# Row sums on one core: the early load of eight rows per partition split in one and seven

## The chip, the cores and the metric

The kernel runs on one core of one Trainium2 chip. The metric is the device time of one execution in microseconds; lower is better. Before the change it is 160.62 us, the median of 3 runs (160.59 to 160.69). The profile comes from one execution of its own.

## The reference

```python
def setup_inputs():
    batch, seq, dim = 32, 512, 1024
    return {"x": np.random.randn(batch, seq, dim).astype(np.float32)}

def reference(x):
    return np.sum(x, axis=-1).astype(np.float32)
```

The input is 16,384 rows of 1,024 float32 (67.1 MB), the output one sum per row (64 KB). There is one addition per element read, so the work is above all reading.

## The kernel before, in words

Each of the 128 partitions gets 128 rows of 4 KB: 16 from the first region of the input (`x_a`) and 112 from the second (`x_b`), consecutive in memory within a region. The rows of a partition are counted from 0 to 127; `rows_from(j, n)` gives rows j to j+n-1 of all partitions. There are three buffers of 16 rows per partition (64 KB), `rows_0` to `rows_2`.

**The loads.** The first one is the early load: rows 112 to 119, eight per partition, 4 MB, into the first half of `rows_0`. It is issued by SyncE (SP, L97). Then follow seven loads of 16 rows per partition (8 MB each, rows 0 to 111), issued by GpSimd (POOL, L99) with `single_packet=True`. The first two of these go into the other two buffers and need no wait; from the third on, POOL waits at L153 until VectorE has summed the buffer that is to be filled again. The last eight rows, 120 to 127, come by four closing loads, again from POOL (L179), cut so that rows 5 and 7 are divided at odd places: `five` has 22,416 B per partition, `seventh` 7,192 B, `sixth` 2,160 B and `eighth` 1,000 B. The pieces `sixth` and `eighth` land in a small tile, `ends`.

**The early load's place.** `issue_first_load_at_entry` (L9 to L27) runs when the program is finalized. It looks for the first DMA that SP issues, takes it out of its block and puts it into the program's entry block, ahead of SP's first drain, which is where the barriers between all engines begin. So this one DMA is issued before the barriers; everything else in the kernel stands behind them. The function moves exactly one DMA and requires that it has no wait.

**The sums.** VectorE (DVE) sums the early load's eight rows and then six of the loads of 16 rows with one `tensor_reduce` each (L106, in `vec`), each behind a wait for that load's semaphore (L172), and each raises `summed`. The seventh load of 16 is shared: DVE sums ten rows with `halves` (L115), a custom instruction that adds the two halves of a row and accumulates, and ScalarE (ACT) sums six with `activation` and its accumulator (L135). The closing rows are shared likewise. ACT stores the sums of the finished rows early (L210, L211), and SP stores the last 16 per partition when DVE's `done` and ACT's `acts` are there (L225 to L227).

**What sets the order.** The order on each engine is that of the program text; there is no scheduler and no pool. DMA transfers of SP go into one queue and those of POOL into another; both are served by the same 16 DMA engines. Each load has a semaphore of its own, which 16 engines raise by one each when their part has landed, so a wait for a whole load is a wait for 16.

Of the kernel before, what the change touches and what calls it, by code (L numbers as in the profile page):

```python
# [30 lines left out]
def kernel(  # L31
# [5 lines left out]
    nc = tc.nc  # L37
# [12 lines left out]
    BIG = 16  # L50
# [15 lines left out]
    def rows_from(j, n):  # L66
        if j < ONE:
            return x_a[:, j : j + n, :]
        return x_b[:, j - ONE : j - ONE + n, :]

    last = J // BIG - 1
    tail = last * BIG
    FIRST = 8
# [14 lines left out]
    def semaphore(name):  # L88
        return ctx.enter_context(nc.semaphore(name=name))

    def block_of(t, a, n):
        return t[:, a * dim : (a + n) * dim].rearrange("p (n d) -> p n d", d=dim)

    def load(dst, src, k):
        sem = semaphore(f"load_{k}")
        if k == "first":
            nc.sync.dma_start(out=dst, in_=src).then_inc(sem, 16)  # L97
        else:
            nc.gpsimd.dma_start(out=dst, in_=src, single_packet=True).then_inc(sem, 16)  # L99
        return sem  # L100

    summed = semaphore("summed")
# [1 line left out]
    def vec(j, block):  # L104
        n = block.shape[1]
        return nc.vector.tensor_reduce(  # L106
            out=sums[:, j : j + n],
            in_=block,
            axis=mybir.AxisListType.X,
            op=mybir.AluOpType.add,  # L110
        )
# [32 lines left out]


    t = bufs[0]
    block = block_of(t, 0, FIRST)
    landed = load(block, rows_from(tail, FIRST), "first")
    loads = [(landed, tail, block)]
    for g in range(last):  # L150
        t = bufs[(1 + g) % 3]
        if g > 1:
            nc.gpsimd.wait_ge(summed, g - 1)  # L153
        block = block_of(t, 0, BIG)
        loads.append((load(block, rows_from(g * BIG, BIG), g), g * BIG, block))

# [2 lines left out]
    j = tail + FIRST  # L161
    t = bufs[(1 + last) % 3]
# [5 lines left out]
    whole6, whole8 = ends[:, :six], ends[:, six:]  # L168
    right6, right8 = whole6[:, 1:-1], whole8[:, 1:-1]
    nc.vector.memset(ends[:, six - 1 :: whole8.shape[-1]], 0.0)  # L170
    for landed, first, block in loads[:-1]:
        nc.vector.wait_ge(landed, 16)  # L172
        vec(first, block).then_inc(summed, 1)
    nc.gpsimd.wait_ge(summed, last - 1)
    line = rows_from(j, 8).rearrange("p n d -> p (n d)")
# [1 line left out]
            (right6, 5 * dim + SIXTH), (right8, 7 * dim + EIGHTH))  # L177
    five, seventh, sixth, eighth = (
        load(dst, line[:, at : at + dst.shape[-1]], f"run_{k}")  # L179
        for k, (dst, at) in enumerate(runs)  # L180
    )
# [3 lines left out]

    paired = semaphore("paired")
    carried = semaphore("carried")
    landed, first, block = loads[-1]
    n_pairs = 10
    nc.vector.wait_ge(landed, 16)  # L190
    for q in range(n_pairs):
# [67 lines left out]
```

## Time and profile before

| | |
|---|---|
| runs (median, lowest, highest) | 160.62 us, 160.59 us, 160.69 us |
| profiled execution, its own time | 160.88 us |
| its span, from SP's first issue to the end of SP's wait for the last store | 159.6 us |
| DVE busy | 121.6 us (76%) |
| ACT busy | 11.0 us (7%) |
| POOL busy | 6.2 us (4%) |
| early load, issue to landing | 24.5 us |
| DVE's first reduce (8 rows), start and length | 24.48 us, 8.7 us |
| DVE's later reduces (16 rows), length of each | 17.2 us |

The span is what the profile's instructions cover; the execution's own time is 1.3 us longer than the span. A load's time from issue to landing contains the time that its packets stand behind others, so it is not the time that the transfer would take alone: the loads of 16 rows need 40.5 us (median) by this count while two of them are under way. Beside the page, the trace holds a record of each instruction, of each DMA packet (queue, start, length, size; not which of the 16 engines moved it) and of each time that a semaphore was raised.

### The profile page before, as it was taken

Reading aid. Unit: us, or ns where it says so; the run is one execution under the profiler, and the core shown is the slowest. Engines: PE = TensorE matmul, PEld = TensorE weight load, DVE = VectorE, ACT = ScalarE, POOL = GpSimd, SP = SyncE. Lnnn points to the kernel's source line nnn. Section 1 sums busy time; section 2 is a strip of 40 time slices with the busy share of each in tenths; the row PEclk is TensorE's granted clock in tenths of the full one; section 3 lists DMA queues with packets and bytes.
Section 4 is the critical chain, followed back from the end, with each engine's and each line's share of the span. In section 5 each row is a group of like instructions: output and inputs, shape, how many; then the busy total and the mean of one; then the engine's idle time right before and its main releaser. Section 6 shows DMA issues by size and latency. Waiting matters only on the chain.

```text
span 159.6 us, 123 instructions
## 1 busy us (share of the span) xinstructions
DVE 121.6 (76%) x42; ACT 11.0 (7%) x19; POOL 6.2 (4%) x15
## 2 busy tenths in 40 slices
DVE  0000008999998999949999499986999679995986
ACT  3000000000000000000000000000000000000995
POOL 3000000010001000010000100010000220000000
DMA  7999996996997979969969969969969979898993
GB/s 263 526 394 394 435 600 279 526 509 279 526 444 345 526 345 444 526 279 509 526 263 526 526 263 526 509 279 526 509 279 526 460 329 526 378 411 364 438 402 127
DMA packets 2000, 67.18 MB, mean 421 GB/s; under 512 B 624, under 2 KB 624, under 8 KB 848
## 3 DMA queue, kind: packets, MB, share of 16 engines
q0 software_dynamic: 1424, 62.92, 91.2%
q1 hardware_dynamic: 288, 4.20, 6.6%
q10 hardware_dynamic: 288, 0.06, 0.2%
HBM read 67.11 MB, written 0.07 MB: 421 GB/s over the span
## 4 chain that ended last, share of the span: by engine, by line
DMA 74%; DVE 22%; POOL 1%; issue 1%; POOLq 0%
DMA rows<-in_x_dram 56%; DVE sums L106 22%; DMA ends<-in_x_dram 19%; POOL rows L99 1%; DVE ends L115 0%; DVE sums L115 0%; POOLq L43 0%
## 5 line engine op out<-in xcount | busy, mean ns | idle before, releaser
L106 DVE TENSOR_REDUCE sums<-rows 128x16 f32<-128x16384 f32 (+1 forms) x7 | 111.9, 15999 | 32.2 <-DMA rows<-in_x_dram 32.2
L135 ACT ACTIVATE unread<-rows 128x1024 f32<-128x1024 f32 x9 | 9.1, 1013 | 145.5 <-DMA rows<-in_x_dram 145.5
L115 DVE CUSTOM_DVE_ANT_0 rows<-rows 128x512 f32<-128x512 f32 (+2 forms) x15 | 9.0, 659 | 2.6 <-DMA rows<-in_x_dram 2.6
L99 POOL DMA_DIRECT2D rows<-in_x_dram x9 | 4.9, 546 | 122.4 <-DVE sums L106 120.9
L135 ACT ACTIVATION_READ_ACCUMULATOR unread<-rows 128x1 f32 x9 | 1.7, 186 | 0.0
L135 ACT ACT_TABLE_LOAD x1 | 1.3, 1283 | 1.4 <-PEq L43 1.4
L170 DVE MEMSET ends<- 128x2 f32 x1 | 0.1, 60 | 1.5 <-PEq L43 1.5
L115 DVE DVE_READ_ACCUMULATOR2_ANT sums<- 128x1 f32 x15 | 1.2, 80 | 0.0
L99 POOL DMA_DIRECT2D ends<-in_x_dram x2 | 1.1, 543 | 0.0
L115 DVE CUSTOM_DVE_ANT_0 ends<-ends 128x271 f32<-128x271 f32 (+1 forms) x2 | 0.7, 364 | 0.1
L115 DVE DVE_READ_ACCUMULATOR2_ANT ends<- 128x1 f32 x2 | 0.2, 84 | 0.0
L243 POOL MEMSET const-float32-0.0<- 128x1 f32 x1 | 0.1, 99 | 0.2 <-issue 0.2
L243 POOL MEMSET const-bfloat16-1.0<- 128x1 bf16 x1 | 0.1, 103 | 0.0
L243 POOL MEMSET const-float32-1.0<- 128x1 f32 x1 | 0.1, 99 | 0.0
L243 POOL MEMSET const-uint8-127<- 128x1 uint8 x1 | 0.1, 99 | 0.0
## 6 DMA issues: line engine op xcount, KB each, us to landing
rows<-in_x_dram SPq DMA_DIRECT2D x1, 4096.0 KB, 24.5
rows<-in_x_dram POOLq DMA_DIRECT2D x1, 2802.0 KB, 27.9
rows<-in_x_dram POOLq DMA_DIRECT2D x1, 899.0 KB, 29.6
ends<-in_x_dram POOLq DMA_DIRECT2D x1, 270.0 KB, 29.7
ends<-in_x_dram POOLq DMA_DIRECT2D x1, 125.0 KB, 29.5
rows<-in_x_dram POOLq DMA_DIRECT2D x7, 40.5
out_dram<-sums ACTq DMA_DIRECT2D x1, 48.0 KB, 1.6
out_dram<-sums ACTq DMA_DIRECT2D x1, 8.0 KB, 1.5
```

Of the source, the lines that this page charges most:

```text
L99: nc.gpsimd.dma_start(out=dst, in_=src, single_packet=True).then_inc(sem, 16)
L106: return nc.vector.tensor_reduce(out=sums[:, j : j + n], in_=block, axis=mybir.AxisListType.X, op=mybir.AluOpType.add,)
L115: return nc.vector.tensor_tensor_reduce(out=src[:, :n], in0=src[:, :n], in1=src[:, n:], scale=1.0, scalar=0.0, op0=mybir.AluOpType.add, op ...
L135: nc.scalar.activation(out=unread[n_acts % len(unread)][:, :], in_=src, func=mybir.ActivationFunctionType.Copy, accum_out=sums[:, j : j + ...
L170: nc.vector.memset(ends[:, six - 1 :: whole8.shape[-1]], 0.0)
L243: nc = _bacc.Bacc("TRN2", target_bir_lowering=False, num_devices=1)
```

## The change

SP's early load becomes two loads on SP: the first of the eight rows per partition (512 KB), and the other seven (3.5 MB). `issue_first_load_at_entry` is unchanged, and it moves only the first DMA of SP; so the load of one row is issued in the entry block ahead of the barriers, and the load of seven rows stands at the head of SP's part of the kernel, behind them. Both raise one semaphore, `entry`, and DVE's first reduce waits for 32 instead of 16. The destination, the rows and the order of everything else are the same; the later loads stay POOL's.

```diff
     def load(dst, src, k):
         sem = semaphore(f"load_{k}")
-        if k == "first":
-            nc.sync.dma_start(out=dst, in_=src).then_inc(sem, 16)
-        else:
-            nc.gpsimd.dma_start(out=dst, in_=src, single_packet=True).then_inc(sem, 16)
+        nc.gpsimd.dma_start(out=dst, in_=src, single_packet=True).then_inc(sem, 16)
         return sem
...
     t = bufs[0]
-    block = block_of(t, 0, FIRST)
-    landed = load(block, rows_from(tail, FIRST), "first")
-    loads = [(landed, tail, block)]
+    entry = semaphore("entry")
+    for j, n in ((0, 1), (1, FIRST - 1)):
+        nc.sync.dma_start(out=block_of(t, j, n), in_=rows_from(tail + j, n)).then_inc(entry, 16)
+    loads = [(entry, 32, tail, block_of(t, 0, FIRST))]
     for g in range(last):
...
-        loads.append((load(block, rows_from(g * BIG, BIG), g), g * BIG, block))
+        loads.append((load(block, rows_from(g * BIG, BIG), g), 16, g * BIG, block))
...
-    for landed, first, block in loads[:-1]:
-        nc.vector.wait_ge(landed, 16)
+    for landed, count, first, block in loads[:-1]:
+        nc.vector.wait_ge(landed, count)
         vec(first, block).then_inc(summed, 1)
...
-    landed, first, block = loads[-1]
+    landed, _, first, block = loads[-1]
```

## Prediction

> **What bounds the kernel now.** I began with the page's table of DMA queues, to see how much of the span the 16 DMA engines are at work:
>
> ```profile
> q0 software_dynamic: 1424, 62.92, 91.2%
> q1 hardware_dynamic: 288, 4.20, 6.6%
> q10 hardware_dynamic: 288, 0.06, 0.2%
> HBM read 67.11 MB, written 0.07 MB: 421 GB/s over the span
> ```
>
> The shares add up to 98.0% of 159.6 us, so all that is not transfer is 3.2 us. q1 is SP's queue (the early load, and the last store), q0 is POOL's. Next the busy time by stretches, to see where those 3.2 us lie (a row: stretch, length, DVE, ACT, POOL, clock, DMA share, GB/s; a transfer counts where it begins):
>
> ```profile
> 0.00:1.00 1.00, 0.00 (x0) 0.00 (x0) 0.20 (x4) 1.00 0.00 0
> 1.00:25.00 24.00, 0.58 (x2) 1.28 (x1) 1.20 (x2) 1.00 1.04 437
> 25.00:50.00 25.00, 25.00 (x2) 0.00 (x0) 0.53 (x1) 1.00 0.97 419
> 50.00:100.00 50.00, 44.95 (x4) 0.00 (x0) 1.59 (x3) 1.00 1.02 440
> 100.00:150.00 50.00, 43.60 (x10) 2.16 (x5) 2.65 (x5) 1.00 0.99 427
> 150.00:157.00 7.00, 6.51 (x23) 6.62 (x14) 0.00 (x0) 1.00 0.94 394
> 157.00:160.00 3.00, 0.98 (x6) 0.90 (x2) 0.00 (x0) 1.00 0.13 23
> ```
>
> They lie in the first microsecond and the last three; in between no engine is ever without work. The chain of work that ended last says the same by its last pieces:
>
> ```profile
> 127.69 29.73 DMA ends<-in_x_dram
> 157.42 0.02 issue
> 157.44 0.04 DVE ends L115
> 157.48 0.33 issue
> 157.81 0.08 DVE sums L115
> ```
>
> Compute follows the last landings within some tenths. The kernel is thus a fixed number of bytes per engine behind a start: it ends when the engine that started last has moved its 4.19 MB. For that start I read the trace's DMA packet records. One of SP's packets is one partition's piece (32,768 B); each of 16 engines has eight, and one closing packet of 4 B that raises the semaphore. The 16 first packets begin 1.02 to 1.54 us after SP's issue at 0.00. They take long, 1.47 to 2.36 us, and end at 2.90 to 3.21 us on 15 engines, at 3.52 on one. From the second on, each takes 1.213 to 1.232 us. So the start-up costs an engine, beyond its first 1.213 us, 1.68 to 1.99 us, and 2.30 us on the last one. That one never catches up: the last of each load's 16 landings is 0.31 to 0.35 us behind the one before it, from the first load (24.46 us against 24.13) to the final one (157.76 against 157.41). **That engine sets the end**, and the others have 0.3 us and more to spare.
>
> The start on the instruction side, by the timeline's first 3 us:
>
> ```profile
> 0.00 0.38 SPq L97 DMA_DIRECT2D rows<-in_x_dram  x1
> ...
> 1.44 1.28 ACT L135 ACT_TABLE_LOAD   x1 [1.44 <-PEq L43]
> 1.51 0.06 DVE L170 MEMSET ends<- 128x2 f32 x1 [1.51 <-PEq L43]
> 1.94 1.20 POOL L99 DMA_DIRECT2D rows<-in_x_dram  x2 [1.50 <-POOLq L43]
> ```
>
> SP issues before the barriers, the others act after them. SP's last barrier event ends at 1.375 us. POOL's first load, issued at 1.94, has its first packet at 6.54 us, so until then only SP's load feeds the engines: four of its packets on each.
>
> **The change, part by part.**
>
> *The packets.* Eight of 32,768 B (8 x 1.213 = 9.70 us per engine) become eight of 4,096 B and eight of 28,672 B, with one more closing packet (9 ns). Neither size occurs before. Near 4,096 B stand 4,320 B at 170 ns and 3,000 B at 127 ns (the closing loads): by the line between them 162 ns. Between 22,416 B (837 ns) and 32,768 B (1,213 ns) a 28,672 B packet takes 1,064 ns. Sum: 8 x 0.162 + 8 x 1.064 + 0.009 = 9.82 us, **+0.12 us** on every engine. If the cost went by bytes alone, at the large packets' rate, it would be 0.01; I take 0.12, since the neighbouring sizes measure it.
>
> *The second issue.* In the changed kernel's order of instructions SP has the 128x1024 copy, the branch with the barriers, the 128x7168 copy, the store: so the change does what it says. The copy's wait is the barrier's, and SP has nothing behind it until the store at 158 us, so nobody queues. Its issue comes at 1.375 us plus a step that the trace has no row for on SP. ACT's step from its last barrier event to its table load is 0.06 us, DVE's to its memset 0.12, POOL's to its first DMA 0.61 (POOL is the far end, as it prepares packets itself). I take ACT's, the other queue that issues through hardware: **1.44 us**. The issue itself, 0.35 to 0.46 us in the four hardware-queue rows, is off the path, as the packets' delay already runs from its beginning.
>
> *Does the entry row cover the way to the second load?* The entry row keeps an engine busy for 1.30 us past its start-up: to 2.98 to 3.29 us on 15 engines, **3.60 us on the last**. The second load flows, with the first load's own delays, at 1.44 + 1.68 to 1.99 = 3.12 to 3.43 us. The 15 could stand idle for some 0.14 us, which their 0.3 us of slack takes up. The last one is covered if its extra 0.31 us are not repeated. I hold that they are not: stretches of one first packet (1.85 to 2.15 us on most, 2.36 there) show once in the trace and at no later change of load or queue. If they are, its data come at 1.44 + 2.30 = 3.74 us and 0.14 us are lost. Below: SP's and ACT's stores have their first packets 0.85 to 0.95 us after issue instead of 1.02, which closes the gap. I take **0**; the ends are a loss of 0.14 us with ACT's step and of 1.98 + 2.30 - 3.60 = 0.68 us with POOL's.
>
> *The start-up itself.* It is the first packet's stretch beyond 1.213 us: 0.64 us on a typical engine, 1.15 on the last. Is it tied to the packet's size? The trace has no second start with idle engines and a load. I take no change, as the cost then is one of time; the closing loads' small packets, 23.5 to 26 B/ns, say that small ones flow no faster. The bound below: with no stretch, the entry row is through at 1.54 + 1.30 = 2.84 us at the latest, and the second load takes over at 1.44 + 1.54 = 2.98 us instead of 3.60: a gain of 0.62 us.
>
> *What else moves.* The first reduce waits for both loads (count 32). They hold the same bytes in the same queue, so it starts near 24.5 us as before. Behind it is POOL's third load at 33.46 us, whose bytes are wanted only when the second ends at 50.4 us; with the 4.6 us from POOL's issue to its first packet there are 12 us of cover. The barriers may come some hundredths earlier if SP's entry issue shrinks; POOL's packets are wanted much later, so that is worth nothing.
>
> *The sum.* 0.12 + 0 + 0 = +0.12 us. On the profiled execution (span 159.58, its time 160.88, 1.30 of it around the span) that is 161.00 us. It ran 0.26 above the median of the runs, and the median carries the forecast: 160.62 + 0.12 = **160.74 us**.
>
> **The rivals.**
>
> *A: the engines run dry behind the entry row (slower).* One mechanism, at the seam near 3 us: SP's second issue is late, or its first packets stretch like the first load's, with only 1.30 us of work in front. It decides when the second load's data reach the latest engine after 3.60 us, that is with an issue after 1.30 us if that engine is slow again, after 1.61 us if the slow 1.99 us of the others hold. With POOL's step it loses 0.68 us: 160.62 + 0.12 + 0.68 = 161.42 us; halfway, 161.1. For it: before, four packets stood there, now one eighth of the load. Against it: ACT's 0.06 us, and the slack of 15 engines. Chance 0.20.
>
> *B: small first packets shorten the start-up (faster).* If a stretch belongs to the large first packet, up to 0.62 us go: 160.62 + 0.12 - 0.62 = 160.12 us. If only the one engine falls in line with the rest, 0.31 go: 160.43. For it: the stretch is seen on first packets only. Against it: nothing shows it to be size and not the cold start. The part of it under 160.30 I give 0.15.
>
> *C: each load pays a fixed cost of its own.* If the second load's packets moved only once the first's completion is through, the last engine would wait from 3.60 us for the 0.35 us between closing packet (first at 23.46) and landing (23.81) and then stretch again by 0.64 to 1.15: +1.0 to 1.5, 161.7 to 162.2 us. Against it: the closing load of 7,192 B per partition lands 2.21 us behind the one before it, and its eight packets of 0.276 us are 2.21 us: nothing is between them. Chance 0.04. The Trainium skill, "DMA: Bandwidth & Descriptors", section "Anatomy of one DMA — SWDGE (gpsimd) path", fits a DMA's time with a constant of about 2.0 us beside its bytes, and its section "Rules for kernel authors" wants at least 1 MiB per DMA, which the 512 KB entry row is not; an estimate that adds that constant once would be about 162.7 us. The trace's 2.21 us speak against adding it for loads that stand queued behind one another.
>
> **How the numbers follow.** 0.2% is 0.32 us, about what a measurement of this kernel can tell from no change; the bounds are 160.30 and 160.94. The forecast has 0.61, from 160.43 (the one engine in line) to 160.88 (its slow start repeated). Slower is A and C, 0.24; faster is B, 0.15. The range reaches into both until a tenth is left out at each end: 160.25 to 161.10 us.
>
> **What would show it.** Right: 16 engines with no idle time between the last 4,096 B packet and the first of 28,672 B; those packets at 0.16 and 1.06 us; SP's second issue at about 1.44 us; the final landing some 0.12 us later. A shows as idle time on the latest engine at 3 to 4 us, and as every landing later by it; B as first packets that take under 0.5 us and landings earlier than 157.76 us; C as idle time of 0.3 us and more on all 16. Wrong altogether would be a change after 30 us, in the closing loads or the stores: there I expect the same intervals as before.

## The result, and the profile after

The changed kernel takes 163.07 us (median of 5 runs, 162.87 to 163.23) against 160.62 us for the kernel before (160.57 to 160.69): a ratio of 1.0153, 95% interval 1.0138 to 1.0167. It is slower by 2.45 us, where 0.12 us had been forecast. The profiled execution took 163.13 us, with a span of 161.8 us.

The table of DMA queues of the changed kernel (packets, MB, share of 16 engines over the span):

```profile
q0 software_dynamic: 1424, 62.92, 90.0%
q1 hardware_dynamic: 432, 4.20, 6.9%
q10 hardware_dynamic: 288, 0.06, 0.2%
HBM read 67.11 MB, written 0.07 MB: 415 GB/s over the span
```

The bytes are the same. The shares add up to 97.1% of 161.8 us, so 4.7 us are without transfer where there were 3.2 us: 1.5 us of idle time are new. The transfers themselves take 157.1 us of an engine instead of 156.4 us: 0.7 us are new there, in packets that take longer. By these shares POOL's queue has 145.6 us in both kernels, so most of the 0.7 us lies in SP's packets.

The chain's last pieces, and the stretches (columns as above):

```profile
129.99 29.68 DMA ends<-in_x_dram
159.66 0.02 issue
159.69 0.04 DVE ends L112
159.72 0.33 issue
160.05 0.08 DVE sums L112
```

```profile
1.00:25.00 24.00, 0.06 (x1) 1.28 (x1) 1.20 (x2) 1.00 1.01 412
25.00:50.00 25.00, 15.96 (x2) 0.00 (x0) 0.53 (x1) 1.00 0.97 422
50.00:100.00 50.00, 50.00 (x4) 0.00 (x0) 1.59 (x3) 1.00 1.01 436
100.00:150.00 50.00, 45.67 (x3) 0.00 (x0) 2.65 (x5) 1.00 0.99 427
```

The end is the old one, 2.3 us later: the same DVE steps behind the same last landing, 160.02 us against 157.76. From 25 us on the engines move as much as before; up to there they move 412 GB/s instead of 437. By the landings: the first load of 16 rows has landed 2.47 us later (34.18 against 31.71), the next 2.30 us (53.36 against 51.06), and the final one 2.26 us. So everything was lost before 32 us, and nothing later.

The start, by the timeline, and the two new loads in the list of DMA issues (KB, us from issue to landing):

```profile
0.00 1.75 SPq L146 DMA_DIRECT2D rows<-in_x_dram  x2
...
1.43 1.28 ACT L132 ACT_TABLE_LOAD   x1 [1.43 <-PEq L43]
1.50 0.06 DVE L168 MEMSET ends<- 128x2 f32 x1 [1.50 <-PEq L43]
1.93 1.20 POOL L96 DMA_DIRECT2D rows<-in_x_dram  x2 [1.49 <-POOLq L43]
34.04 8.69 DVE L103 TENSOR_REDUCE sums<-rows 128x8 f32<-128x8192 f32 x1 [32.48 <-DMA rows<-in_x_dram]
```

```profile
rows<-in_x_dram SPq DMA_DIRECT2D x1, 3584.0 KB, 32.6
rows<-in_x_dram SPq DMA_DIRECT2D x1, 512.0 KB, 3.5
```

The 1.75 us are two issues of 0.36 and 0.33 us with the barriers between them; the second begins at 1.42 us, as forecast (1.44). The row lands 3.5 us after its issue. The seven rows land 32.6 us after theirs. DVE's first reduce starts 9.6 us later for that (34.04 us instead of 24.48), and it costs nothing: DVE then reduces without a pause until 111 us and has caught up.

What happens in between shows first in the stretch from 3 to 4 us (columns as above; a transfer counts where it begins), in the kernel before and then in the changed one:

```profile
3.00:4.00 1.00, 0.00 (x0) 0.00 (x0) 0.15 (x1) 1.00 0.84 360
```

```profile
3.00:4.00 1.00, 0.00 (x0) 0.00 (x0) 0.13 (x1) 1.00 0.28 90
```

Few transfers begin there in the changed kernel, 90 GB/s instead of 360. The packet records tell more. The row's closing packets come at 2.73 to 3.22 us. The first packets of the seven rows come at 2.73 to 3.22 us on five engines, and at 3.9 to 4.9 us on the others. So most engines stand idle, for 0.8 to 2.2 us, and their first packet of 28,672 B then takes up to 0.93 us longer than the 1.062 us of the later ones. (The records don't name the engine; which packets follow one another on one engine is worked out from their times.) I sum this up for each run by two numbers, worked out from the packet records: idle time, and stretch (what packets took beyond the time of their size in the stream), both from 0 to 32 us and as a mean of the 16 engines. The idle time of the kernel before is the way to the first packets.

| kernel | idle | stretch | sum | last landing |
|---|---|---|---|---|
| before | 1.1 us | 0.7 us | 1.8 us | 157.76 us |
| changed | 2.3 us | 1.4 us | 3.7 us | 160.02 us |

The sum is 1.9 us more. The rest of the 2.26 us is spread: the final load's first and last landing lie 1.85 us apart (158.17, 160.02), before 0.65 us, and the last one counts.

### The profile page after: what moved, and what is told of

The parts are those of the page before. It is cut to its first block, busy times and chain, and to the rows that moved or that the text cites. A ratio compares the mean times of both kernels' runs of the same rounds, so it can differ in the third digit from the quotient of the medians.

```text
span 161.8 us, 124 instructions
## 1 busy us (share of the span) xinstructions
DVE 121.3 (75%) x42; ACT 11.0 (7%) x19; POOL 6.2 (4%) x15
## 4 chain that ended last, share of the span: by engine, by line
DMA 60%; DVE 37%; POOL 1%; issue 1%
DMA rows<-in_x_dram 41%; DVE sums L103 37%; DMA ends<-in_x_dram 18%; POOL rows L96 1%; DVE ends L112 0%; DVE sums L112 0%
## 6 DMA issues: line engine op xcount, KB each, us to landing
rows<-in_x_dram SPq DMA_DIRECT2D x1, 3584.0 KB, 32.6
```

## The experiments

The runs were made in four jobs. Each job ran the kernel before beside its kernels, and the ratios are to that. The theories have numbers or letters that hold for the run at hand; they are not the rivals A, B and C of the prediction.

**First job: the split, the place, the cover, the company.** The theories were: (1) the one row is too little work to cover the second load's way; (2) the split itself costs; (3) the second load is slowed by POOL and ACT, which start beside it.

*Both loads at the entry (e1).* The helper moves SP's first two DMAs, not the first alone.

```diff
-        at = next((k for k, i in enumerate(insts) if isinstance(i, mybir.InstDMACopy) and i.engine == SP), None)
+        at = [k for k, i in enumerate(insts) if isinstance(i, mybir.InstDMACopy) and i.engine == SP][:2]
...
-        main.instructions = entry[:k] + [load] + entry[k:]
+        main.instructions = entry[:k] + loads + entry[k:]
```

> One row and seven rows as in the changed kernel, but both of SP's loads stand in the entry block, so the second is issued behind the first at about 0.4 us and not behind the barriers. Theory 1 (the one row covers 1.3 us of work, and the second load's first packets come up to 2.7 us or more after an issue at 1.42 us, with a stretch of 0.4 to 0.95 us on top): the second issue is a microsecond earlier, its packets are there when the row is through (2.7 to 3.2 us) on nearly all engines, 160.4 to 161.0 us. Theory 2 (two loads, small packets or the shared semaphore cost this wherever they stand): about 163 us. Theory 3 (the second load is slow because it starts while POOL writes its packets and ACT loads its table, 1.4 to 3.1 us): 160.4 to 161.0 us, as theory 1.

Measured 160.56 us, ratio 0.9997 (0.9988 to 1.0006). The timeline:

```profile
0.00 0.84 SPq L143 DMA_DIRECT2D rows<-in_x_dram  x2
...
2.40 1.20 POOL L93 DMA_DIRECT2D rows<-in_x_dram  x2 [1.96 <-POOLq L40]
```

The second issue ends at 0.84 us, the barriers come 0.5 us later for it, and POOL's first load with them (2.40 instead of 1.93); that costs nothing. The first packets of the seven rows come at 2.5 to 3.25 us and follow the row's without a gap. So the split, the sizes and the shared semaphore cost nothing. Theory 2 is out.

*Nothing at the entry (e2).* The kernel before without the line `nc.at_finalize(issue_first_load_at_entry)`.

> The kernel before, but its eight-row load is left in its place behind the barriers. Theory 1 (what costs is a seam behind a short first load): there is no seam; everything starts 1.42 us later, 160.62 + 1.42 = 162.0 us, which is better than the changed kernel. Theory 2 (the split costs): also 162.0 us. Theory 3 (a load issued at 1.4 us is slow because of what runs beside it): first packets at 2.7 to 4.9 us instead of 2.4 to 3.0, 163 us or more.

Measured 162.03 us, ratio 1.0085 (1.0071 to 1.0099). SP issues at 1.39 us, beside the table load at 1.40:

```profile
1.39 0.38 SPq L96 DMA_DIRECT2D rows<-in_x_dram  x1
1.40 1.28 ACT L134 ACT_TABLE_LOAD   x1 [1.40 <-PEq L42]
```

All 16 first packets begin at 2.39 to 2.81 us, 1.0 to 1.4 us after the issue, and their stretch is 0.70 us, as with the early load. A load issued at 1.4 us to idle engines is not slow. And the row that the changed kernel loads early gains it nothing: without any early load this kernel is no slower.

*Four rows and four (e3).*

```diff
-    for j, n in ((0, 1), (1, FIRST - 1)):
+    for j, n in ((0, 4), (4, FIRST - 4)):
```

> The changed kernel with four rows at the entry and four behind the barriers. Theory 1: four rows are about 5 us of work per engine, to 6.6 us or later, and the second load's packets are there by 4.9 us at the latest: no idle time, 160.6 to 160.8 us. Theory 2: about 163 us. Theory 3: the second load may be slow, but four rows cover it, 160.6 to 160.8 us.

Measured 160.63 us, ratio 1.0000 (0.9991 to 1.0009). There is no idle time behind the start. With four rows in front, the barriers' place does no harm.

*POOL's first load behind the row's landing (e4).* SP's two loads get a semaphore each, DVE waits for both, and

```diff
+        if g == 0:
+            nc.gpsimd.wait_ge(row, 16)
```

> The changed kernel with a semaphore for each of SP's two loads, and POOL's first load waits until the one row has landed (3.5 us), so that POOL writes no packets while the second load starts. POOL's packets are still in time, as seven rows keep the engines busy for 8 us. Theory 1: no change from the changed kernel, 162.8 to 163.3 us. Theory 2: the same. Theory 3, as far as POOL's issue is what runs beside it: the second load's first packets at 2.4 to 3.1 us on all engines, 160.6 to 161.3 us.

Measured 162.26 us, ratio 1.0101 (1.0087 to 1.0115). That is 0.8 us less than the changed kernel in its own job, so I took POOL's issue for a part of the cause, although the first packets of the seven rows still came as late as some 4.2 us, with 0.7 us of new idle time. The last job shows that this was wrong.

**Second job: which delay?** Theory A: a load issued while the engines move data needs 2.5 us and more to its first packets. Theory B: the packets arrive in time, but SP's queue, running empty, takes them up in a second start.

*Four rows by ACT (e5).*

```diff
-    for j, n in ((0, 1), (1, FIRST - 1)):
-        nc.sync.dma_start(out=block_of(t, j, n), in_=rows_from(tail + j, n)).then_inc(entry, 16)
+    for issuer, j, n in ((nc.sync, 0, 4), (nc.scalar, 4, FIRST - 4)):
+        issuer.dma_start(out=block_of(t, j, n), in_=rows_from(tail + j, n)).then_inc(entry, 16)
```

> Four rows at the entry by SP, the other four behind the barriers by ACT, whose queue is another one: the 16 engines take turns between the two queues, so the first packet of ACT's load shows when its packets have arrived while SP's packets flow. Theory A (any load issued while the engines are moving data needs 2.5 to 3.5 us to its first packet): first packets at 3.9 to 4.9 us. Theory B (packets arrive within 1.0 to 1.5 us as always, but a queue that is just running empty takes them up only in a second start): 2.4 to 3.2 us, up to 0.6 us later by the packet that is under way. The time is that of the kernel before in both, 160.5 to 160.8 us.

Measured 160.57 us, ratio 0.9997 (0.9987 to 1.0006). ACT issues at 1.43 us, and its first packets come from 5.1 us on, up to 6.3 us: 3.7 to 4.9 us after the issue, in a queue of its own, while the packets of the other queue (0.61 us each) follow one another. Theory B as it stood is out; the delay is even longer than theory A had it. The engines had packets of SP to move all the while (no idle time), so this run can't tell late packets from packets that stand in line.

*Seven rows by ACT (e6).* As e5, with one row and seven.

> One row at the entry by SP, the seven others behind the barriers by ACT, in a queue that has not run before. Theory A: as the changed kernel, first packets of the seven rows at 2.7 to 4.9 us, 162.5 to 163.3 us. Theory B: first packets at 2.4 to 3.2 us, little idle time, 160.6 to 161.3 us.

Measured 161.93 us, ratio 1.0087 (1.0072 to 1.0102). First packets from 2.6 us on, 0.5 us of new idle time. Another queue doesn't heal the seam; the time fits neither expectation.

*Two rows and six (e7).* The pairs are (0, 2) and (2, 6).

> The changed kernel with two rows at the entry and six behind the barriers: the two rows keep the engines busy to 4.0 to 4.4 us. Theory A: packets of the second load arrive at 2.7 to 4.9 us, so idle time of 0 to 0.6 us on some engines, 160.6 to 161.5 us. Theory B: the packets are there well before the queue runs empty, no idle time, 160.5 to 160.8 us.

Measured 161.86 us, ratio 1.0088 (1.0064 to 1.0111): above both ranges. The six rows' first packets come from 3.8 us on, with a mean of 0.25 us of idle time, and the stretch sums to 1.1 us.

*The seven rows issued only when the row has landed (e8).*

```diff
+        if j:
+            nc.sync.wait_ge(row, 16)
```

> The changed kernel with a semaphore for each of SP's loads, and SP issues the seven rows only when the one row has landed (3.25 us), that is 1.8 us later, at engines that stand idle. Theory A: a load that is issued to idle engines has its first packets after 1.0 us, at 4.3 to 4.6, with a stretch of 0.6 us; so the later issue costs little, 162.5 to 163.3 us, the changed kernel's time. Theory B: the same, as the changed kernel's second load makes a second start too. If instead the changed kernel's loss were the lateness of its issue alone, 1.8 us would be added, 164.9 us.

Measured 161.85 us, ratio 1.0074 (1.0058 to 1.0091), below both ranges. The timeline says what fills the gap:

```profile
0.00 3.53 SPq L148 DMA_DIRECT2D rows<-in_x_dram  x2
...
1.95 1.20 POOL L96 DMA_DIRECT2D rows<-in_x_dram  x2 [1.51 <-POOLq L43]
```

SP's second issue now comes at 3.2 us. POOL's first load, issued at 1.95 us as ever, with nothing in front of it but the rest of the one row (through by 2.9 us), has its first packets at 3.33 to 4.17 us, 1.4 to 2.2 us after its issue; before the change, behind eight rows, they came at 6.54 to 7.16 us, 4.6 to 5.2 us after it. SP's seven rows are now behind POOL's load: they begin at 8.8 us, 5.6 us after their issue, when each engine has moved two of POOL's 64 KB packets. So POOL's 4.6 us were for the most part not POOL's own: they were the wait behind the load in front. Since POOL's load had been issued before SP's second one, the run doesn't show what a second load of SP needs with nothing in front of it; e15 below does.

**Third job: the dose, and the delay away from the start.**

*Three rows and five (e9).*

> The changed kernel with three rows at the entry and five behind the barriers. One row lost 2.45 us and two rows 1.23 us, a difference of 1.22 us, which is one more row's work; so the second load takes over at the same moment, some 5.3 us, whatever stands in front (theory A: a load issued while the engines move data needs that long). Three rows end near 5.3 us: nothing or 0.1 us is lost, 160.6 to 160.8 us. Theory B (every seam in SP's queue with the barriers in between costs a start of its own) gives a third loss of some 0.6 us, 161.2 us.

Measured 160.55 us, ratio 0.9995 (0.9986 to 1.0004), with no idle time. Three rows are enough. So, by the medians and by rows at the entry, the loss is: none 1.5 us (e2), one 1.7 to 2.5, two 1.2, three 0.

*Seven rows by ACT and POOL late (e10)*, the edits of e6 and e4 together.

> One row at the entry by SP, seven behind the barriers by ACT, and POOL's first load waits until the one row has landed: the two changes that each took part of the loss away (0.8 us and 1.1 us), together. Theory C (POOL's issue beside it and SP's queue still running are two separate delays of the second load): both parts go, some 161.2 us. Theory A (a load issued into running transfers is late whatever the queue, and what is left is the second start): no better than the better of the two alone, 161.8 to 162.0 us.

Measured 162.10 us, ratio 1.0093 (1.0077 to 1.0108). The two supposed parts don't add: it is 0.1 us above theory A's range, and 0.9 us above theory C's time.

*The table load held back (e11).*

```diff
+    nc.scalar.wait_ge(loads[1][0], 16)
+    nc.scalar.wait_ge(summed, 1)
+    nc.scalar.activation(out=spare[:, :], in_=sums[:, tail : tail + 1], func=mybir.ActivationFunctionType.Copy)
```

> The changed kernel, with ACT's table load held back: ACT first waits until DVE has summed the early rows, and copies one column of sums into a tile of its own that nobody reads, so the 1.28 us of the table load lie at about 43 us and not at 1.42 to 2.71 us, beside the second load's start. If the table load takes part in the delay, the first packets of the seven rows come before 3.9 us on more than 5 engines and the time falls, to 162.5 us or below; if not, 162.8 to 163.3 us.

Measured 162.20 us, ratio 1.0105 (1.0085 to 1.0125), single runs from 161.76 to 162.97. By what was expected this spoke for the table load: the time is below the bound, and the first packets of the seven rows come before 3.9 us on all engines but one. But the changed kernel itself has nearly as much of both in the last job (e13), and e14 below settles it.

*A probe in the stream (e12).* The kernel before, with one small load more:

```diff
+    nc.scalar.wait_ge(loads[4][0], 16)
+    nc.scalar.dma_start(out=probe[:, :], in_=x_r[:P, :16]).then_inc(probed, 16)
+    nc.scalar.wait_ge(probed, 16)
```

> The kernel before, with one more load: ACT loads 64 B per partition into a tile that nobody reads, issued when POOL's fourth load has landed (89.8 us), in the midst of the stream. Its packets show how long a load takes to its first packet while the engines are busy. Theory A: 2.5 us or more to the first packet, up to 4.9 us as in the start. Theory D (only the first microseconds are slow, when everything starts at once): 1.0 us and the rest of the packet under way, 1.0 to 3.4 us. The time is that of the kernel before within 0.1 us.

The timeline of ACT, and the probe in the list of issues:

```profile
89.49 0.37 ACTq L189 DMA_DIRECT2D probe<-in_x_dram  x1
147.68 1.28 ACT L135 ACT_TABLE_LOAD   x1 [147.68 <-DMA rows<-in_x_dram]
148.97 1.03 ACT L135 ACTIVATE unread<-rows 128x1024 f32<-128x1024 f32 x1
```

```profile
probe<-in_x_dram ACTq DMA_DIRECT2D x1, 8.0 KB, 21.8
```

Its first packets come at 93.53 to 93.89 us, 4.0 to 4.4 us after the issue. That lies outside theory D's 3.4 us, in the steady stream, far from the start. In that time an engine ends the 64 KB packet that it has in hand and moves one more. The eight packets of an engine then come one at a time, 2.42 us apart, each behind one of POOL's 64 KB packets, which is why 8 KB need 21.8 us to land. The time was 161.27 us, ratio 1.0041 (1.0026 to 1.0055), not the time of the kernel before: my waits also pushed the table load to 147.68 us, ahead of the six activations, and ACT ended late.

**Fourth job: is the company a part of it?** The company is what runs beside the second load's start: POOL's issue and ACT's table load. The changed kernel ran once more, in one job and on one chip with the three kernels that follow it.

*The changed kernel again (e13).*

> The changed kernel as it is, on the chip of the three that follow. If the gains of the late POOL issue and of the late table load are real: 162.9 to 163.2 us, and those two below it by 0.8 us. If they are scatter from job to job: some 162.2 us, as they have.

Measured 162.31 us (162.02 to 162.67), ratio 1.0110 (1.0095 to 1.0125): 0.8 us less than in the first measurement, and outside its interval. The other kernels with one row at the entry and seven behind it (e4, e6, e10, e11 above, e16 and e14 below) lie between 161.93 and 162.26 us, so the first measurement is the one that stands apart: of its 2.45 us, 1.7 us came again. The new idle time is 0.6 us here, where it was 1.2 us.

*POOL late again (e16).*

> The changed kernel with POOL's first load behind the landing of the one row, once more: 162.0 to 162.4 us. Theory C (POOL's packets written beside it delay the second load): below the changed kernel on this chip by some 0.8 us. Theory A (the running transfers delay it): the same as the changed kernel on this chip, within 0.4 us.

Measured 162.23 us, ratio 1.0111 (1.0097 to 1.0126). On one chip, the late POOL issue gains nothing that stands out of the scatter of single runs. The 0.8 us of e4 were a difference between jobs.

*POOL and the table load both out of the way (e14)*, the edits of e4 and e11.

> The changed kernel with POOL's first load behind the landing of the one row and the table load at about 43 us, so that nothing but the one row's own transfers runs beside the second load's issue. Theory C (the company is the cause): first packets of the seven rows at 2.4 to 3.0 us on all engines, idle time below 0.2 us, 160.7 to 161.2 us. Theory A (transfers that flow delay a newly issued load): first packets still as late as 4 us on several engines, 161.6 to 162.3 us.

Measured 162.13 us, ratio 1.0092 (1.0077 to 1.0107). In the timeline, the first 3.6 us hold SP's two loads and nothing beside them:

```profile
0.00 1.75 SPq L146 DMA_DIRECT2D rows<-in_x_dram  x2
...
3.61 1.20 POOL L96 DMA_DIRECT2D rows<-in_x_dram  x2 [3.17 <-DMA rows<-in_x_dram]
```

Still the engines stand idle for a mean of 0.60 us between 2.5 and 6 us, the same as the changed kernel in this job (0.59), and stretch 0.97 us (0.94). Theory 3 and this run's theory C are out.

*A tiny load at the entry (e15)*, 64 B per partition into an unread tile, with all eight rows behind the barriers.

> The kernel before with its eight rows behind the barriers, and in the entry block a load of 64 B per partition into a tile that nobody reads: SP's queue has run, but no transfers flow when the eight rows are issued. Theory A: the eight rows start as with nothing at the entry, first packets at 2.4 to 2.8 us, 162.0 us. Theory E (a second load in a queue that has just run is late, whatever flows): first packets later than 3.5 us on several engines, 163 us or more.

Measured 162.06 us, ratio 1.0091 (1.0078 to 1.0104), e2's time. The issues:

```profile
0.00 0.37 SPq L150 DMA_DIRECT2D spare<-in_x_dram  x1
...
1.42 0.33 SPq L97 DMA_DIRECT2D rows<-in_x_dram  x1
```

The tiny load's packets begin at 0.98 to 1.03 us and take some 10 ns each, so none is left at 1.42 us. The eight rows' first packets come at 2.37 to 2.84 us on 15 engines, 3.42 on one, 0.95 to 2.0 us after the issue. A queue that has just run is not slow; a load that is not yet through is what matters. Theory E is out.

How far the load in front has got seems to matter little. POOL's first load is issued at 1.93 us here and at 1.90 us in e2 (the instruction takes 0.67 us), while the eight rows' packets begin at 2.37 us or later; still it waits until 6.4 us or later, behind three packets of SP on each engine.

## Why the prediction was wrong

*The step that failed* is this one: "The second load flows, with the first load's own delays, at 1.44 + 1.68 to 1.99 = 3.12 to 3.43 us." It took the delay of a load with nothing in front of it for that of a load issued behind one that is still running. Measured: the first packets at 2.73 to 4.9 us, 1.3 to 3.5 us after the issue, instead of 2.46 to 2.98, and a second stretch on top, so that most engines were in flow at 4.7 us or later. The ends that I had bounded it with, ACT's and POOL's steps to the issue, concerned the wrong quantity, since the issue came at 1.42 us, as taken. The row that shows the right one was in the trace of before, and I quoted it: POOL's load, issued at 1.94 us, with its first packet at 6.54. I read that as POOL's own slowness. It was the nearest row for a load issued behind a running one, and with it the gap would have been seen: a second load that takes until 1.42 + 4.6 = 6.0 us, with work until 3.60, loses up to 2.4 us. That this bound lies so near the 2.45 us measured is luck: behind one row the wait was 1.1 to 3.5 us (the changed kernel, e13 and e14), not 4.6.

*Rival A* named the right mechanism at the right place, with too small a price: 0.68 us at most, by the time of the issue. That the engines run dry is shown (e3, e9 and e1 remove the idle time, and the loss with it). That the second load is late because the row in front of it is still running, and not for SP's queue, POOL, ACT or the moment of the issue, is shown by e14 (no company, still late), e6 (another queue, still late), and e2 and e15 (the same moment with nothing in front, not late). That loads issued behind others wait elsewhere too is shown by e5, e8 and e12, but there the engines were busy. The size is only roughly accounted for: 1.2 us of new idle time and 0.7 us of stretch on the mean, the rest in the engines' spread.

*Rival B* had its part: the row's small first packets stretched by 0.3 us instead of 0.7, and the row was through at 2.73 to 3.22 us instead of 2.98 to 3.60. In the changed kernel that only made the gap wider. Without a gap (e1) it gave no time that can be measured.

*Rival C* is refuted: in e1 and e3 a second load follows the first at no cost. The 2.0 us that the formula of the Trainium skill ("DMA: Bandwidth & Descriptors", section "Anatomy of one DMA — SWDGE (gpsimd) path") would have added come near to the 2.45 measured, but by no such cost; the page states it for loads that GpSimd issues, and the second load is SP's.

*The last engine that sets the end* is no fixed thing. In the traces of e1, e3, e9 and of e12, whose early load is that of the kernel before, the last landing is 0.03 to 0.08 us behind the one before it, not 0.31 to 0.35; in e5 it is 0.18 us, and in the two traces of the changed kernel 0.35 and 0.38 us. So 0.3 us of my cover was an accident of one profile.

*The packets* cost 0.159 and 1.062 us, where I had 0.162 and 1.064: 8 x 0.159 + 8 x 1.062 + 0.009 = 9.78, 0.07 us more than before, where I had 0.12. The second issue at 1.42 us, the harmless barriers and the unchanged end came as forecast.

*The first reduce* did not: I had it near 24.5 us, "as before", and it started at 34.04. Once POOL's packets come, the engines take turns between the two queues packet by packet. Before, four of SP's eight packets on each engine had gone by then; in the changed kernel it was two of the eight packets of the seven rows on the mean, and each of the others waits for one of POOL's 64 KB packets. That it doesn't need the gap is shown by e9 and e3: without idle time their first reduce starts at 31.34 and 36.32 us. That it does no harm was right: POOL's third load is issued at 43.02 us instead of 33.46, 10 us before the second one has landed (53.36).

*What stays open* is why packets wait behind a load that is still running: whether they reach the engines late, or the engines have already taken on other packets for some microseconds. The records tell only when a packet begins. The second can't be all of it: in the changed kernel's gap the engines had no other packets to move. Open, too, is why two measurements of the changed kernel lie 0.8 us apart.

## What to carry to other kernels

The time from a DMA's issue to its first packets depends on what was issued ahead of it and is not yet through: with nothing ahead it was 1.0 to 2.0 us here, behind one row 1.1 to 3.5 us, behind loads that kept the engines busy 3.7 to 5.6 us and more. So a short load in front of a long one must hold work for the longer time: here three rows, 1.5 MB, did and two did not. Look in the trace for a load that was issued behind a running one, on whatever queue, before taking the start's delay for it. Before a part of a loss is put down to one cause, run the changed kernel itself in the same job: a gain of 0.8 us between two jobs was none.

## What the runs showed of the hardware

- With nothing in front of it, a load of SP had its first packets after 1.0 to 1.4 us (e2) and 0.95 to 2.0 us (e15). Behind one row it was 1.1 to 3.5 us, with idle engines in between (the changed kernel, e13, e14). Behind longer loads, ACT's needed 3.7 to 4.9 us (e5) and 4.0 to 4.4 us (e12), SP's 5.6 us (e8). The Trainium skill, "DMA: Bandwidth & Descriptors", section "Latency and other measured facts", gives some 600 ns to the first byte for DMAs of SP and ACT; every run here has more, and the stream several times that.
- Engines take turns between queues packet by packet, so the packets' size sets the waiting: 64 B packets waited 2.42 us each behind 64 KB packets (e12).
- Kernels with the gap scatter from run to run, 162.02 to 162.67 us (e13) or 161.38 to 162.38 us (e14), while those without it keep within 160.46 to 160.68 us (e9).
